# GLA's exponents as a pipe part of their own, and GLA and retention in one pipe

## The chip, the cores and the metric

The kernel runs on one core of one Trainium2 chip. The metric is the device time of one execution in microseconds (us). Three executions of the kernel before took 2648.84, 2644.02 and 2642.16 us; the median is 2644.02 us.

## The reference

Two transformer blocks on a sequence of 1024 rows of 1024 channels, in float32. The first block mixes tokens with two mixers side by side, retention (512 channels, 4 heads) and gated linear attention, GLA (512 channels, 4 heads with keys of 64), and then applies an MLP. The change touches the token mixer of this first block alone. Cut to what matters, GLA is, for each chunk of 64 rows:

```python
b = jnp.cumsum(lai, axis=1)
decay = jnp.exp(-jnp.abs(b[:, :, None] - b[:, None, :]))
A = jnp.einsum('bthd,bshd,btshd->bhts', qi, ki, decay)
o = jnp.einsum('bhts,bshe->bthe', A, vi)
o = o + jnp.einsum('bthd,bhde->bthe', qi * jnp.exp(b), state)
new_state = jnp.exp(b_last)[..., None] * state + jnp.einsum(
    'bshd,bshe->bhde', ki * jnp.exp(b_last[:, None] - b), vi)
```

The decay depends on the channel and on both rows, so it does not factor into one matmul. Both mixers end in a norm per head and a gate; the two results are put side by side and multiplied by `w_out`. The second block (SSD, S5 and RG-LRU mixers, cross attention, an MLP) is not touched.

## The kernel before

Every large product in float32 is made of three matmuls on split operands (`mm3`, L114 to L116: high by high, high by low, low by high), one for each 128 rows of the contraction, on a [128, 512] result. An operand is split by ACT (L82, a cast) and DVE (L83, the rest). Tiles come from pools with a fixed number of buffers (`BUFS`: 8 pages each of the kinds H and X, 8 of W, 4 of U, 6 of S; two PSUM tiles each of the kinds mm, tr and sc). The program is written as Python generators; the Tile framework takes the order in which instructions are written as their priority and fixes each engine's order by its own cost model. Engines wait for each other by semaphores, each engine keeps its own order, and so does each queue of DMAs.

The sequence is cut into 8 blocks of 128 rows. The stage of the change works so:

- `gla_proj` writes GLA's query, key and cumulated gate (`g_qkb`), its values (`gv`) and its output gate (`gg`) to DRAM.
- `ret_proj` makes retention's gate (`rg`, 8 tiles) and query and key (`r_qk`, 16 tiles) with 24 matmuls for each tile. It yields after every tile.
- `gla_block(i)` does one block of GLA in three parts. **Part one** loads values, gate and `g_qkb` (`vg`, `qkb`, pages H), and for j = 0, 1 makes seven levels of exponents: POOL subtracts (L562, seven instructions of 128x128), ACT takes the absolute value and the exponential (L564, L565, 128x896), DVE multiplies by the query (L567, into a second page X), POOL by the key (L568, in place). Then TensorE multiplies the levels (L575; two groups g = 0, 1 for each j, 16 matmuls of 64 rows each, into an sc tile), and DVE assembles the matrix A from the levels (L580 once and L583, a copy under a mask, 7 times for each j). **Part two** scales query and key for the state (L591 to L595), multiplies by the state and by A (L598, L600), transposes the keys (L604), copies them (L606, ACT), multiplies them with the values (L609) and updates the state (L614, DVE). Then it takes the norm's statistics (`head_norm`: L485, L486, small operations at L491, L492, L135 and L143 to L148, all on DVE) and scales the result (L503 on ACT). **Part three** gates it (L506, POOL), transposes it (L509, TensorE), scales it (L477, ACT) and writes it to DRAM (`g_od`).
- `pipe` starts one block more in each step and lets every live block do one part; it takes the newest block first unless `oldest` is set. `weave(main, side, n)` lets the side do n steps for each step of the main generator. Here the main is `ret_proj` and the side is the pipe of GLA blocks with n = 0.3.
- Behind it stand `ret_setup` (tables, and the weights of retention's values), a broadcast of the gate, `wout_load` (L703, POOL, and splits) and a second pipe, of `ret_block(i)`: its first part loads `r_qk` twice, makes the values with 24 matmuls, rotates (L662 POOL, L663 and L664 DVE), multiplies query by key (L668), masks (L669 DVE) and transposes (L673); its second part makes the output and the state (L679, L680, L682, L685), and norm and gate follow as in GLA.

A step below is the stretch from one block's first L575 to the next block's.

Of the kernel before, what the change touches and what calls it, by code (L numbers as in the profile page):

```python
# [17 lines left out]
NB = 8  # L18
# [377 lines left out]
def _rows(ap, t):  # L396
    return ap[t * 128:(t + 1) * 128, :]


class Mix1(Net):  # L400
# [110 lines left out]

    def pipe(self, gens, oldest=False):

        live, gens, d = [], list(gens), 1 if oldest else -1
        while gens or live:
            if gens:
                live.append(gens.pop(0))
            live = [g for g in live[::d] if next(g, self) is not self][::d]
            yield

# [26 lines left out]
    def gla_block(self, i):  # L547
        nc = self.nc
        sl = slice(128 * i, 128 * i + 128)
        vg = self.page("H")  # L550
        nc.sync.dma_start(out=vg[:, 0:512], in_=_rows(self.g_vd, i))
        nc.sync.dma_start(out=vg[:, 512:1024], in_=_rows(self.g_gd, i))
        qkb = self.page("H")[:, 0:768].rearrange("p (s j c) -> p s j c", s=3, c=128)
        nc.sync.dma_start(out=qkb, in_=self.g_qkb[:, :, :, sl])
        A = self.half([128, 2, 2, 128])
        for j in range(2):
            q, k, b = qkb[:, 0, j, :], qkb[:, 1, j, :], qkb[:, 2, j, :]
            E = self.page("X")[:, 0:896].rearrange("p (l c) -> p l c", c=128)
            for l in range(7):
                w = 64 >> l  # L560
                bv = b.rearrange("p (g c) -> p g c", c=2 * w)
                nc.gpsimd.tensor_tensor(out=E[:, l, :].rearrange("p (g c) -> p g c", c=2 * w), in0=bv,  # L562
                                        in1=bv[:, :, w - 1:w].broadcast_to([128, 64 // w, 2 * w]), op=ALU.subtract)
            nc.scalar.activation(out=E, in_=E, func=ACTF.Abs)  # L564
            nc.scalar.activation(out=E, in_=E, func=ACTF.Exp, scale=-0.0625)  # L565
            qt = self.page("X")[:, 0:896].rearrange("p (l c) -> p l c", c=128)
            nc.vector.tensor_tensor(out=qt, in0=E, in1=q.unsqueeze(1).broadcast_to([128, 7, 128]), op=ALU.mult)  # L567
            nc.gpsimd.tensor_tensor(out=E, in0=E, in1=k.unsqueeze(1).broadcast_to([128, 7, 128]), op=ALU.mult)  # L568
            for g in range(2):
                ps = self.ps("sc").rearrange("p (r u c) -> p r u c", r=2, c=128)  # L570
                for u in range(4):
                    l = 4 * g + u - 1
                    for r in range(2):
                        rs = slice(64 * r, 64 * r + 64)
                        nc.tensor.matmul(out=ps[:, r, u, :], lhsT=k[rs] if l < 0 else E[rs, l, :],  # L575
                                         rhs=q[rs] if l < 0 else qt[rs, l, :], start=True, stop=True)
                for u in range(4):
                    l = 4 * g + u - 1
                    if l < 0:
                        nc.vector.tensor_tensor(out=A[:, j], in0=ps[:, :, u, :], op=ALU.mult,  # L580
                                                in1=self.ident.unsqueeze(1).broadcast_to([128, 2, 128]))
                    else:
                        nc.vector.copy_predicated(out=A[:, j], data=ps[:, :, u, :],  # L583
                                                  mask=self.gmask[:, l, :].unsqueeze(1).broadcast_to([128, 2, 128]))
# [12 lines left out]
        for j in range(2):  # L597
            nc.tensor.matmul(out=o[:, 2 * j:2 * j + 2, :], lhsT=qd[:, j, :], rhs=self.g_S[j], start=True, stop=False)  # L598
            for h in (2 * j, 2 * j + 1):
                nc.tensor.matmul(out=o[:, h, :], lhsT=A[:, j, h % 2, :], rhs=vg[:, h * 128:(h + 1) * 128],  # L600
                                 start=False, stop=h % 2 == 1)
# [45 lines left out]
    def ret_block(self, i, T):  # L647
# [16 lines left out]
        nc.vector.tensor_tensor(out=qk, in0=qk, in1=sw, op=ALU.add)  # L664
        A, kT = sw[:, 0], sw[:, 1]
        ps = self.ps("tr").rearrange("p (h c) -> p h c", c=128)
# [1200 lines left out]
def build(tc, I, out):  # L1867
    from contextlib import ExitStack
    with ExitStack() as ctx:
        n = Mix2(tc, ctx, I, out)  # L1870
        n.modulation()
        n.kv_mem()
        def run(g):
            while True:
                try:
                    next(g)
                except StopIteration as e:
                    return e.value
# [7 lines left out]
        T, steps = None, [3, 0, 1, 0, 1]  # L1886
        while T is None:
# [4 lines left out]
            T = next(norm)  # L1892
# [5 lines left out]
            yield from n.s5_setup()  # L1898
        run(n.weave(n.gla_proj(T), early(), 0.75))
        n.gla_setup()  # L1900
        run(n.weave(n.ret_proj(T), n.pipe(n.gla_block(i) for i in range(NB)), 0.3))
        n.ret_setup()
        n.gate1 = n.bcast(n.mod["gate1"][0])
        n.wout = n.wout_load(I["w_out"], n.gate1, (4, 6))
        run(n.pipe(n.ret_block(i, T) for i in range(NB)))
        T = run(n.block1_out())
        T = n.block1_mlp(T)
        n.dt_proj(T)
# [9 lines left out]
        out = n.block2_out()  # L1918
        T = next(out)
        run(n.weave(n.pipe(n.ssd_block(i) for i in range(NB)), delay(out, 3)))  # L1920
        T = run(n.attention(T))
# [87 lines left out]
```

## Time and profile before

| what | value |
|---|---|
| median of three runs | 2644.02 us |
| the profiled execution | 2643.23 us, span 2641.4 us |
| TensorE busy, share of the span | 2536.1 us, 96% |
| mean granted TensorE clock | 0.982 |
| TensorE busy from 205 to 620 us | 370.82 of 415 us, clock 0.95 |
| TensorE busy from 620 to 2641 us | 1984.41 of 2021 us, clock 1.00 |

The stage of the change lies between about 300 and 620 us of the span. The granted clock has two levels here, 1.0 (2.4 GHz) and 0.5 (1.2 GHz); a value between them is the mean of a stretch that holds both.

### The profile page before, as it was taken

The numbers are of one execution on the slowest core, as the hardware profiler recorded it, in microseconds if no ns is written. First come the engines' busy times: TensorE is split into PE (matmuls) and PEld (weight loads), VectorE is DVE, ScalarE is ACT, GpSimd is POOL, SyncE is SP. The second block draws the span as 40 slices with busy tenths as digits, with TensorE's granted clock in tenths as the row PEclk, the third lists the DMA queues.
The fourth block names the chain that finished last, engine by engine and source line by source line (L and its number), as shares of the span: only waits on it lengthen the run. The fifth ranks groups of instructions, "written<-read, shape, count | busy, mean of one in ns | idle before, by whom it ended". The sixth has DMA issues, their size and how long they took to land. (4 is left out here: it accounts for less than half of the span.)

```text
span 2641.4 us, 32947 instructions
## 1 busy us (share of the span) xinstructions
PE 2536.1 (96%) x12086; PEld 2061.0 (78%) x12086; DVE 1877.5 (71%) x3177; ACT 1165.0 (44%) x1834; POOL 240.6 (9%) x222
## 2 busy tenths in 40 slices
PE   7899989889999999999999998999999999999997
PEld 7586777677888888888877776778887888888886
DVE  4857666688898777647775468786557977777786
ACT  3622233344654444433553474652227444434342
POOL 4121135541000000000000003100000000000000
PEclk8899999999999999999999999999999999999999
DMA  9772433465166569966632334371102765799783
GB/s 327 254 266 100 144 104 96 132 163 167 61 215 236 192 218 330 325 193 223 209 128 85 106 102 133 118 246 40 56 17 84 271 218 193 257 339 333 269 281 106
DMA packets 255130, 484.36 MB, mean 183 GB/s; under 512 B 21604, under 2 KB 110964, under 8 KB 254968
## 3 DMA queue, kind: packets, MB, share of 16 engines
q1 hardware_dynamic: 247768, 470.59, 52.6%
q10 hardware_dynamic: 7200, 11.67, 1.2%
q8 instruction: 95, 1.56, 0.2%
q14 instruction: 67, 0.55, 0.1%
HBM read 338.80 MB, written 143.38 MB: 183 GB/s over the span
## 5 line engine op out<-in xcount | busy, mean ns | idle before, releaser
L114 PE MATMUL ps<-W,H 128*128 128x512 f32 x1088 | 424.8, 390 | 0.3 <-ACT H L82 0.2
L116 PE MATMUL ps<-W,H 128*128 128x512 f32 x1088 | 424.2, 390 | 0.0
L115 PE MATMUL ps<-W,H 128*128 128x512 f32 x1088 | 423.9, 390 | 0.0
L83 DVE TENSOR_TENSOR W<-S,W 128x1024 fp32r<-128x1024 f32 (+1 forms) x271 | 332.2, 1230 | 127.6 <-ACT W L82 126.7
L114 PE MATMUL ps<-U,W 128*128 128x512 f32 (+1 forms) x1064 | 419.4, 394 | 2.5 <-ACT W L82 2.2
L115 PE MATMUL ps<-U,W 128*128 128x512 f32 (+1 forms) x1064 | 417.4, 392 | 1.5 <-DVE U L372 1.5
L116 PE MATMUL ps<-U,W 128*128 128x512 f32 (+1 forms) x1064 | 416.1, 391 | 0.8 <-DVE W L83 0.8
L82 ACT CAST W<-S 128x1024 fp32r<-128x1024 f32 x287 | 297.0, 1042 | 241.5 <-PE ps L115 155.4
L83 DVE TENSOR_TENSOR H<-S,H 128x1024 fp32r<-128x1024 f32 x131 | 159.9, 1221 | 150.3 <-ACT H L82 145.5
L82 ACT CAST H<-S 128x1024 fp32r<-128x1024 f32 x131 | 137.5, 1050 | 279.9 <-PE ps L115 197.9
L114 PEld LDWEIGHTS ps<-W,H 128*128 128x128 f32 x1088 | 204.3, 188 | 43.5 <-DVE X L1106 0.8
L114 PEld LDWEIGHTS ps<-U,W 128*128 128x128 f32 (+1 forms) x1064 | 197.0, 185 | 51.1 <-ACT W L82 3.4
L116 PEld LDWEIGHTS ps<-W,H 128*128 128x128 f32 x1088 | 204.2, 188 | 41.8
L115 PEld LDWEIGHTS ps<-W,H 128*128 128x128 f32 x1088 | 204.3, 188 | 41.6
L115 PEld LDWEIGHTS ps<-U,W 128*128 128x128 f32 (+1 forms) x1064 | 197.2, 185 | 48.3 <-DVE U L372 4.6
L116 PEld LDWEIGHTS ps<-U,W 128*128 128x128 f32 (+1 forms) x1064 | 197.0, 185 | 45.7 <-DVE W L83 1.9
L116 PE MATMUL ps<-W,U 128*128 128x512 f32 x352 | 140.7, 400 | 5.3 <-DVE U L83 5.3
L114 PE MATMUL ps<-W,U 128*128 128x512 f32 x352 | 142.3, 404 | 2.3 <-DVE X L305 2.0
L115 PE MATMUL ps<-W,U 128*128 128x512 f32 x352 | 141.2, 401 | 0.0
L807 ACT ACTIVATE ev<-ev 128x512 f32<-128x512 f32 x104 | 65.3, 629 | 135.2 <-DVE ev L905 110.3
L116 PEld LDWEIGHTS ps<-W,U 128*128 128x128 f32 x352 | 67.5, 192 | 20.7 <-DVE U L83 6.6
L808 ACT ACTIVATE X<-ev 128x512 f32<-128x512 f32 x126 | 79.8, 634 | 3.4
(546 smaller groups left out, 4523.3 us busy)
## 6 DMA issues: line engine op xcount, KB each, us to landing
S<-mlp_h SPq DMA_DIRECT2D x112, 512.0 KB, 5.0
S<-in_w_ff SPq DMA_DIRECT2D x96, 512.0 KB, 5.2
mlp_h<-X SPq DMA_DIRECT2D x96, 512.0 KB, 3.8
S<-in_mlp_w SPq DMA_DIRECT2D x96, 512.0 KB, 5.1
mlp_w<-S SPq DMA_DIRECT2D x96, 256.0 KB, 2.8
S<-mlp_w SPq DMA_DIRECT2D x48, 512.0 KB, 4.8
S<-in_w_in SPq DMA_DIRECT2D x46, 512.0 KB, 5.4
X<-in_w_ada SPq DMA_DIRECT2D x32, 512.0 KB, 6.8
```

The costliest lines, as they stand in the source:

```text
L82: self.nc.scalar.copy(out=hi, in_=src)
L83: (lo_eng or self.nc.vector).tensor_tensor(out=lo, in0=src, in1=hi.bitcast(F32), op=ALU.subtract)
L114: mm(out=ps, lhsT=lh, rhs=rh, start=start and k == 0, stop=False)
L115: mm(out=ps, lhsT=lh, rhs=rl, start=False, stop=False)
L116: mm(out=ps, lhsT=ll, rhs=rh, start=False, stop=stop and k == n - 1)
L807: nc.scalar.activation(out=r, in_=x, func=ACTF.Relu)
L808: nc.scalar.activation(out=out, in_=r, func=ACTF.Square)
```

## The change

`gla_block` gets four parts. The new first part loads `qkb` alone and makes the exponents and both products for j = 0 and 1, and keeps them in `Es`. The second part loads values and gate and holds the matmuls, now at L583, and the copies, now at L588 and L591. The other two parts are as they were. Lines behind the edit stand 8 further on in the changed program (L598 is L606, L604 is L612, L609 is L617, L595 is L603, L668 is L676, L673 is L681, L679 is L687); L506, L509, L562 to L568 stay.

`pipe` now takes its blocks from an iterator as it goes, and is called with `oldest` set. The two pipes are one: the generator `blocks` gives the eight GLA blocks, an empty one, then runs what is left of `ret_proj`, does the setups and `wout_load`, gives another empty one and then the eight retention blocks. It is woven with `ret_proj` at 0.42 in place of 0.3.

```diff
     def pipe(self, gens, oldest=False):
 
-        live, gens, d = [], list(gens), 1 if oldest else -1
-        while gens or live:
-            if gens:
-                live.append(gens.pop(0))
+        live, gens, d = [], iter(gens), 1 if oldest else -1
+        while True:
+            g = next(gens, None)
+            if g is not None:
+                live.append(g)
+            elif not live:
+                return
             live = [g for g in live[::d] if next(g, self) is not self][::d]
             yield
...
-        vg = self.page("H")
-        nc.sync.dma_start(out=vg[:, 0:512], in_=_rows(self.g_vd, i))
-        nc.sync.dma_start(out=vg[:, 512:1024], in_=_rows(self.g_gd, i))
         qkb = self.page("H")[:, 0:768].rearrange("p (s j c) -> p s j c", s=3, c=128)
         nc.sync.dma_start(out=qkb, in_=self.g_qkb[:, :, :, sl])
-        A = self.half([128, 2, 2, 128])
+        Es = []
...
+            Es.append((E, qt))
+        yield
+        vg = self.page("H")
+        nc.sync.dma_start(out=vg[:, 0:512], in_=_rows(self.g_vd, i))
+        nc.sync.dma_start(out=vg[:, 512:1024], in_=_rows(self.g_gd, i))
+        A = self.half([128, 2, 2, 128])
+        for j in range(2):
+            q, k, (E, qt) = qkb[:, 0, j, :], qkb[:, 1, j, :], Es[j]
...
-        run(n.weave(n.ret_proj(T), n.pipe(n.gla_block(i) for i in range(NB)), 0.3))
-        n.ret_setup()
-        n.gate1 = n.bcast(n.mod["gate1"][0])
-        n.wout = n.wout_load(I["w_out"], n.gate1, (4, 6))
-        run(n.pipe(n.ret_block(i, T) for i in range(NB)))
+        proj = n.ret_proj(T)
+
+        def blocks():
+            for i in range(NB):
+                yield n.gla_block(i)
+            yield iter(())
+            run(proj)
+            n.ret_setup()
+            n.gate1 = n.bcast(n.mod["gate1"][0])
+            n.wout = n.wout_load(I["w_out"], n.gate1, (4, 6))
+            yield iter(())
+            for i in range(NB):
+                yield n.ret_block(i, T)
+
+        run(n.weave(proj, n.pipe(blocks(), True), 0.42))
```

DVE before, in the third block's step (X_3141 and X_3180 are the products of that block's successor, `half_2887` is the matrix A that is assembled, `ps_2901` to `ps_2953` are its four groups):

```order
L148 SCALAR_TENSOR_TENSOR sm_2743<-rs_2744,sm_2743 128x4
L567 TENSOR_TENSOR X_3141<-X_3131,H_3128 128x896
L567 TENSOR_TENSOR X_3180<-X_3170,H_3128 128x896
L580 TENSOR_TENSOR half_2887<-ps_2901,ident 128x256
L583 COPY_PREDICATED half_2887<-half_2298,ps_2901 128x256 x3
L583 COPY_PREDICATED half_2887<-half_2298,ps_2914 128x256 x4
L580 TENSOR_TENSOR half_2887<-ps_2940,ident 128x256
L583 COPY_PREDICATED half_2887<-half_2298,ps_2940 128x256 x3
L583 COPY_PREDICATED half_2887<-half_2298,ps_2953 128x256 x2
```

DVE now, in the same block's step (`half_2948` is its A, `ps_2962` to `ps_2988` are its last three groups, X_3216 and X_3229 are products of the block two further on):

```order
L591 COPY_PREDICATED half_2948<-half_2298,ps_2962 128x256 x2
L588 TENSOR_TENSOR half_2948<-ps_2975,ident 128x256
L591 COPY_PREDICATED half_2948<-half_2298,ps_2975 128x256
L567 TENSOR_TENSOR X_3216<-X_3206,H_3204 128x896
L591 COPY_PREDICATED half_2948<-half_2298,ps_2975 128x256 x2
L591 COPY_PREDICATED half_2948<-half_2298,ps_2988 128x256 x4
L567 TENSOR_TENSOR X_3229<-X_3219,H_3204 128x896
L83 TENSOR_TENSOR W_3505<-S_3503,W_3504 128x1024
L83 TENSOR_TENSOR W_3511<-S_3509,W_3510 128x1024
L485 BN_STATS st_3122<-ps_3104 128x6 x2
```

The two products moved from ahead of the copies of the block before them into the copies of the block two before them, and ahead of a norm's statistics.

POOL before, two neighbouring steps (H_2966, H_3209 and H_3452 at L506 are the gated outputs, H_3371 and H_3642 are two blocks' `qkb`):

```order
L506 TENSOR_TENSOR H_2966<-H_2966,H_2620 128x512
L595 TENSOR_TENSOR H_3209<-H_3209,H_2885 128x256
L562 TENSOR_TENSOR X_3374<-H_3371 128x128 x7
L562 TENSOR_TENSOR X_3413<-H_3371 128x128 x7
L568 TENSOR_TENSOR X_3374<-X_3374,H_3371 128x896
L568 TENSOR_TENSOR X_3413<-X_3413,H_3371 128x896
L595 TENSOR_TENSOR H_3452<-H_3452,H_3128 128x256
L506 TENSOR_TENSOR H_3209<-H_3209,H_2882 128x512
```

POOL now, one step (H_3447 at L603 belongs to the block after the one in L506's turn, H_3893 is the last block's `qkb`):

```order
L603 TENSOR_TENSOR H_3785<-H_3785,H_3447 128x256
L506 TENSOR_TENSOR H_3554<-H_3554,H_3391 128x512
L562 TENSOR_TENSOR X_3895<-H_3893 128x128 x7
L568 TENSOR_TENSOR X_3895<-X_3895,H_3893 128x896
L562 TENSOR_TENSOR X_3908<-H_3893 128x128 x7
L568 TENSOR_TENSOR X_3908<-X_3908,H_3893 128x896
```

Where both sets of subtractions stood ahead of both products, the second set now stands behind the first product, and all of them behind L506.

TensorE before, the matmuls of the levels in one step (U and W are operands of `ret_proj`):

```order
L575 MATMUL ps_3144<-H_3128 128x128 x2
L575 MATMUL ps_3144<-X_3141,X_3131 128x128 x6
L575 MATMUL ps_3157<-X_3141,X_3131 128x128 x8
L604 MATMUL ps_3224<-ident,H_3209 128x128 x2
L114 MATMUL ps_3272<-U_613,W_3058 128x512
L575 MATMUL ps_3183<-H_3128 128x128 x2
L575 MATMUL ps_3183<-X_3180,X_3170 128x128 x6
L575 MATMUL ps_3196<-X_3180,X_3170 128x128 x8
```

TensorE now, from the last of twelve matmuls of `ret_proj` behind the first group (`ps_3165`, `ps_3178` and `ps_3191` are the other three groups of the same block):

```order
L115 MATMUL ps_3244<-U_614,W_3233 128x512
L583 MATMUL ps_3165<-X_3013,X_3003 128x128 x8
L583 MATMUL ps_3178<-H_3001 128x128 x2
L583 MATMUL ps_3178<-X_3026,X_3016 128x128 x6
L116 MATMUL ps_3244<-U_613,W_3234 128x512
L114 MATMUL ps_3244<-U_613,W_3239 128x512
L115 MATMUL ps_3244<-U_614,W_3239 128x512
L583 MATMUL ps_3191<-X_3026,X_3016 128x128 x8
```

The single matmul between the two j became twelve between the groups of j = 0, none between j = 0 and j = 1, and three between the groups of j = 1. Between one block's first group and the next block's stood 96, 72, 72, 96, 72 and 7 of these matmuls from the second block on, and now 48, 48, 72, 48, 72 and 48. The first L676 of retention stands behind the last GLA block's products with the state, as L668 did.

## Rows read from the trace of the kernel before

**Rows 1.** Busy time by windows of the span; columns as the first line says.

```profile
core 0: us, PE busy (x) PEld busy (x) DVE busy (x) ACT busy (x) POOL busy (x), PEclk, DMA share, GB/s
205.00:620.00 415.00, 370.82 (x2149) 302.21 (x2148) 290.03 (x831) 143.55 (x301) 144.06 (x151) 0.95 0.42 128
620.00:2641.00 2021.00, 1984.41 (x9059) 1613.33 (x9057) 1460.34 (x2180) 936.97 (x1426) 35.73 (x26) 1.00 0.54 185
```

**Rows 2.** TensorE's waits, 205 to 620 us: total us, times, longest.

```profile
PE ps L575 <- DVE half L583: 23.2, 11, 6.9
PE ps L668 <- DVE H L664: 4.3, 3, 2.2
```

**Rows 3.** Timeline from 380 us: start, us, engine, line, operation, [idle before <-releaser].

```profile
379.91 0.39 PE L116 MATMUL ps<-U,W 128*128 128x512 f32 x1
380.14 0.39 PE L114 MATMUL ps<-U,W 128*128 128x512 f32 x1
...
381.78 5.11 POOL L562 TENSOR_TENSOR X<-H 128x128 f32<-128x128 f32 x14 [5.32 <-DMA H<-g_qkb]
...
386.76 1.09 DVE L567 TENSOR_TENSOR X<-X,H 128x896 f32<-128x896 f32 x1 [9.21 <-ACT X L565]
...
387.93 2.08 POOL L568 TENSOR_TENSOR X<-X,H 128x896 f32<-128x896 f32 x1 [1.03 <-DVE X L567]
...
388.96 1.99 DVE L567 TENSOR_TENSOR X<-X,H 128x896 f32<-128x896 f32 x1 [1.12 <-ACT X L565]
...
392.86 0.80 PE L575 MATMUL ps<-H 64*128 64x128 f32 x4 [4.53 <-DVE half L583]
```

**Rows 4.** Windows as in 1: a long wait and the stretch behind it, thrice.

```profile
387.90:392.80 4.90, 0.43 (x3) 0.11 (x1) 3.65 (x5) 1.80 (x3) 3.85 (x2) 0.75 0.14 54
392.80:397.10 4.30, 4.24 (x33) 3.88 (x34) 3.67 (x9) 0.00 (x0) 0.30 (x1) 0.50 0.00 0
418.60:422.50 3.90, 0.44 (x3) 0.12 (x1) 3.70 (x5) 0.58 (x2) 3.90 (x2) 0.82 0.61 202
422.50:427.90 5.40, 5.35 (x35) 4.80 (x36) 4.43 (x10) 0.00 (x0) 4.71 (x3) 0.50 0.01 3
480.50:487.50 7.00, 0.52 (x3) 0.20 (x2) 6.90 (x7) 3.17 (x5) 4.27 (x3) 0.89 0.40 121
487.50:492.80 5.30, 4.92 (x25) 4.06 (x25) 4.62 (x10) 0.80 (x4) 4.20 (x2) 0.50 0.55 179
```

**Rows 5.** Window as in 1: one step without a long wait.

```profile
360.00:386.00 26.00, 24.64 (x163) 20.31 (x163) 14.19 (x41) 8.14 (x19) 7.61 (x15) 1.00 0.33 107
```

**Rows 6.** Groups: busy us, mean ns of one | idle before, releasers.

```profile
L506 POOL TENSOR_TENSOR H<-H,H 128x512 f32<-128x512 f32 x16 | 23.4, 1462 | 39.9 <-ACT H L503 23.9 <-ACT H L500 16.0
L562 POOL TENSOR_TENSOR X<-H 128x128 f32<-128x128 f32 x91 | 35.2, 426 | 90.2 <-PE ps L575 61.6 <-DMA H<-g_qkb 16.3 <-DVE s5t L1467 12.3
L564 ACT ACTIVATE X<-X 128x896 f32<-128x896 f32 x12 | 11.4, 953 | 44.3 <-POOL X L562 44.3
L567 DVE TENSOR_TENSOR X<-X,H 128x896 f32<-128x896 f32 x12 | 18.3, 1527 | 51.8 <-ACT X L565 51.8
L583 DVE COPY_PREDICATED half<-half,ps 128x256 f32<-128x256 uint8 x112 | 49.4, 443 | 5.7 <-PE ps L575 1.7
L485 DVE BATCH_NORM_STATS2 st<-ps 128x6 f32<-128x128 f32 x32 | 8.0, 287 | 0.1
L491 DVE TENSOR_TENSOR sm<-sm 128x4 f32<-128x4 f32 x8 | 1.3, 157 | 0.0
L503 ACT ACTIVATE H<-ps,sm 128x128 f32<-128x128 f32 x25 | 7.2, 369 | 5.8 <-DVE sm L148 5.8
L83 DVE TENSOR_TENSOR W<-S,W 128x1024 fp32r<-128x1024 f32 x12 | 18.9, 1584 | 6.2 <-ACT W L82 6.2
```

**Rows 7.** DMA issues, 300 to 620 us: times, KB each, median us to landing.

```profile
g_od<-H SPq DMA_DIRECT2D x8, 256.0 KB, 3.0
H<-g_qkb SPq DMA_DIRECT2D x5, 384.0 KB, 5.2
```

## The prediction

> **What bounds the kernel now.** I read the windows of busy time first, then TensorE's waits inside the stretch they point to, then the timeline around the longest of them. From 620 us on TensorE is busy 1984.4 of 2021 us at full clock, so nothing is to be had there; from 205 to 620 us it is busy 370.8 of 415 us at a clock of 0.95 [rows 1]. Those 44.2 idle us and the half clock are all that this change can touch. More than half of the idle time is one wait: L575, the matmuls of GLA's levels, for L583, the copies that free its PSUM tile, 23.2 us in 11 waits, the longest 6.9 [rows 2].
>
> The copies are not slow themselves. In the timeline POOL begins the next block's subtractions at 381.78, late because its `qkb` had only just landed. ACT's functions follow, DVE makes the next block's product of j = 0 from 386.76 and that of j = 1 until 390.95. Only then may DVE copy the groups of the present block, for which TensorE has been waiting, since DVE's order puts both products ahead of the copies; TensorE goes on at 392.86 after 4.53 us [rows 3]. So a late exponent stops TensorE not as an operand, for it is the next block's, but through the copies queued behind it. This happens three times. The three waits leave 4.90 - 0.43 = 4.47, 3.90 - 0.44 = 3.46 and 7.00 - 0.52 = 6.48 us idle, and behind each of them TensorE runs at a granted clock of 0.50, the lower of the two levels, for 4.24, 5.35 and 4.92 busy us, half of which is lost [rows 4]. A step without such a wait stands at full clock throughout [rows 5].
>
> **What is removed.** The three waits and the half clock behind them: 14.4 + (4.24 + 5.35 + 4.92) / 2 = 14.4 + 7.3 = 21.7 us [rows 4]. In the new order the copies of j = 0 stand ahead of both products, so a late exponent no longer holds the groups that TensorE wants next; I count all of it as gone. The eight shorter waits that make up the rest of the 23.2 us, some 8 us, may shrink, as twelve matmuls now cover the first group's copies; but where the ring below sets the step that pays nothing, so I count none of it and keep 8 us as the bound.
>
> **What is added: a loop over the engines.** The new DVE order puts L567 of block k+2 amid the copies of block k and ahead of the norm's statistics, and the new POOL order puts the subtractions of k+2 behind L506 of block k-1, the second set behind L568 of the first. That closes a ring with one turn for each step: statistics on DVE, L503 on ACT, L506, L562, ACT, L567, L568, L562, ACT, L567, statistics. Its length by the means [rows 6]: the DVE tail is 26 instructions, 8 for the statistics at up to 0.287, 8 copies and state updates at up to 0.443, 10 small ones from 0.157, 7.4 us at these prices, and I take 7.0 since the statistics' second kind is shorter; L503 4 x 0.369 = 1.48; L506 1.46; seven L562 at 0.426 = 2.98, twice; ACT 2 x 0.953 = 1.91, twice; L567 1.53, twice; L568 2.08 [rows 3]. The sum is 24.9 us. With the shortest that the timeline shows, L562 at 5.11 / 14 = 0.365 and L567 at 1.09 [rows 3], it is 23.1. I take 24.0, the middle, since L562 and L567 will run in part alone.
>
> TensorE's own step: the undisturbed one took 26.0 us with 72 matmuls of `ret_proj` [rows 5]. These follow each other by 380.14 - 379.91 = 0.23 us [rows 3], so a step with 48 takes 26.0 - 24 x 0.23 = 20.5. The steps in which exponents are still made have 48, 48, 72, 48 and 72. In the three short ones the ring is longer by 24.0 - 20.5 = 3.5 us, together 10.5. If the two long ones' slack of 2.0 each could be used it would be 5 x 24.0 - (3 x 20.5 + 2 x 26.0) = 6.5. I take 8.5. By the ends of the ring, 23.1 and 24.9, this term runs from 2.0 to 13.2.
>
> In two of the five steps a pair of weight splits (L83) stands behind the second L567 and ahead of the statistics, 2 x 1.58 = 3.2 us more in the ring [rows 6]; it counts in full in the second step (48 matmuls) and less 2.0 of slack in the fifth (72): 4.4 us. In the second step the wait so becomes 3.5 + 3.2 = 6.7 us, longer than two of the three waits behind which the half clock stood; I charge it one such stretch, half of 5.35, 2.7 us [rows 4].
>
> What row is there on who holds DVE? L567 took 1.09 us alone and 1.99 us where it began while POOL's L568, from 387.93 to 390.01, was under way; it ended 0.94 us behind it [rows 3]. The Trainium skill (SBUF — State Buffer, "SBUF: two separate sides") says that a VectorE operation with two SBUF inputs and a GpSimd operation take one shared port pair as a lock for the whole instruction. The trace agrees. By that rule L567 would always run alone in the new order, as L568 waits for it, the ring would stand near its short end, 23.1, and the sum below would be some 2.7 us better, an estimate. The same rule speaks against the change at the splits, which now follow L567 at once and so run beside L568: up to 2.08 us more in each of two steps, some 4 us worse, and together 1 us worse than my sum.
>
> **What is only moved.** Loading values and gate in the second part moves two DMAs of 256 KB on SP's queue behind `qkb`; they are wanted a step later, at L608, and cost nothing while SP isn't blocked. Retention's first L676 still stands behind the last GLA block's output, so the single pipe weaves little. In retention's blocks two matmuls of the values, not some twenty, now stand between transposes and L687, which exposes the mask on DVE. The bounds are a gain of the 4.3 us that L668 waits for L664 now [rows 2] and a loss of 8 x 0.7, the copy of one group and more, 5.6 us; I take nothing, as both lie about equally near.
>
> **The sum**: 21.7 - 8.5 - 4.4 - 2.7 = 6.1 us gained. Against the profiled execution, 2643.2, this is 2637.1 us; the median of the runs is 0.8 higher, and I forecast 2637.5. That lies at the edge of what a measurement of this kernel can tell from no change, about 0.3% or 7.9 us.
>
> **Rivals.**
> 1. *The ring never binds.* POOL need not wait for L506 where the statistics came early, and a step's lead is spent before the ring catches up. Then the 21.7 us are gained in full, and half of the eight short waits' 8 us: 2643.2 - 25.7 = 2617.5 us. For it: DVE is idle for 51.8 us in front of L567 today, all for ACT [rows 6], time which the new order could fill. Against it: the new order is a chain with few gaps.
> 2. *Slower: the load of `qkb` ends last.* POOL already stood 16.3 us for `qkb` [rows 6]. The page for block k+2's `qkb` comes free when block k-2 has been written out, on the same SP queue: 3.0 + 5.2 = 8.2 us from one issue to the other's landing [rows 7]. If that lands behind L506 of step k by 4.5 us, somewhat less than the 5.32 that POOL stood idle ahead of 381.78 [rows 3], the ring grows to 28.5 and, as L567 stands in the copies, TensorE stops with it: 5 x 4.5 = 22.5 us, 2660 us. It decides from the point at which the load lands later than L506 begins. Against it: a whole group of matmuls stands between the block's last transpose and the next step.
> 3. *The change doesn't do what it says*: the exponents gain a step, but DVE's and POOL's fixed orders hand the wait on one to one, and nothing is woven. Then waits of 3 to 7 us stay in other places: 2640 to 2648, say 2644 us.
>
> **How the numbers follow.** Forecast 0.50, within it 2629 to 2647 from the bounds of the ring and of retention; rival 1 0.20; rival 2 0.13; rival 3 0.17. Faster than 2636.1: rival 1 and a little under half of the forecast, 0.20 + 0.24 = 0.44. Slower than 2651.9: rival 2 and a little of the others, 0.15. Between: 0.41. The range reaches half into rival 1 and not to rival 2's full price: 2616 to 2655 us leaves out about one in ten on each side.
>
> **What would show it.** In the changed profile L567 should no longer wait some 10 us for ACT with TensorE idle; the wait of L583 for L591 should be shorter than 23.2 us and without the three long ones; the clock behind a block's first groups should be 1.00, not 0.50. The ring is right if steps with 48 matmuls take about 24 us and those with 72 about 26. Steps of 20.5 us would show rival 1; POOL idle in front of L562 for `qkb` in every step, and steps of 28 us, rival 2. An unchanged sum of idle time, in other waits, would show rival 3. I would be wrong altogether if the time moved outside 300 to 620 us.

## The result, and the profile after

The changed kernel took 2661.88 us (median of four runs, 2659.29 to 2664.44) against 2643.64 us before: a ratio of 1.0067, with a 95% interval of 1.0055 to 1.0080. It is slower by 18 us. The forecast was 6 us faster, and the time lies above the top of the stated range, 2655 us.

The windows say where. The columns are those of [rows 1]; first the changed kernel, then the kernel before.

```profile
300.00:520.00 220.00, 197.26 (x1183) 154.96 (x1182) 145.45 (x349) 75.30 (x145) 95.01 (x119) 0.95 0.35 113
520.00:640.00 120.00, 98.52 (x543) 82.78 (x542) 73.57 (x209) 45.60 (x121) 39.98 (x24) 0.93 0.59 152
640.00:1000.00 360.00, 359.65 (x1602) 294.46 (x1601) 297.81 (x510) 180.48 (x279) 0.00 (x0) 1.00 0.51 178
```

```profile
300.00:520.00 220.00, 194.49 (x1209) 159.38 (x1207) 140.55 (x354) 72.96 (x138) 97.13 (x118) 0.95 0.35 114
520.00:640.00 120.00, 106.25 (x604) 89.46 (x605) 91.98 (x247) 52.62 (x138) 42.16 (x25) 0.97 0.65 178
```

Behind 640 us TensorE is busy at full clock, as it was before [rows 1], so what was lost was lost ahead of it: in GLA's stretch 26 fewer matmuls in the same 220 us, and in retention's 61 fewer in 120 us, at a mean clock of 0.93 in place of 0.97. The long waits of [rows 2] are gone, and others stand in their place. TensorE's waits in the changed kernel from 205 to 640 us (total us, times, longest):

```profile
PE ps L509 <- POOL H L506: 19.7, 9, 3.3
PE ps L617 <- ACT H L614: 6.7, 3, 3.1
PE ps L583 <- DVE half L591: 6.6, 10, 1.6
PE ps L617 <- DVE half L622: 5.4, 7, 2.0
```

Two of them can be followed on the timeline (start, us, engine, line, operation). In GLA, the transposes of the keys (L612) are done, and the state matmul L617 stands on TensorE's queue almost behind them; but the copy L614 that it needs stands on ACT behind two casts, a copy for the projection and the four scalings of the block before:

```profile
377.06 1.98 ACT L82 CAST W<-S 128x1024 fp32r<-128x1024 f32 x2
...
377.27 1.09 DVE L567 TENSOR_TENSOR X<-X,H 128x896 f32<-128x896 f32 x1 [4.30 <-ACT X L565]
...
377.55 0.38 PE L612 MATMUL ps<-ident,H 128*128 128x128 f32 x2
...
377.86 0.49 PE L583 MATMUL ps<-H 64*128 64x128 f32 x4
...
378.27 4.23 DVE L83 TENSOR_TENSOR W<-S,W 128x1024 fp32r<-128x1024 f32 x2
378.44 2.99 POOL L568 TENSOR_TENSOR X<-X,H 128x896 f32<-128x896 f32 x1 [3.58 <-DVE X L567]
378.95 0.58 ACT L640 COPY ev<-ps 128x512 f32<-128x512 f32 x1
...
379.98 0.88 ACT L477 ACTIVATE H<-ps,norm_w 128x128 f32<-128x128 f32 x3 [0.18 <-issue]
...
380.75 0.38 ACT L614 COPY H<-ps 128x256 f32<-128x256 f32 x1
...
381.18 0.70 PE L617 MATMUL ps<-H,H 128*128 128x256 f32 x2 [2.39 <-ACT H L614]
...
384.92 1.22 PE L617 MATMUL ps<-H,H 128*128 128x256 f32 x2 [1.97 <-DVE half L622]
```

TensorE is busy 1.75 of the 3.70 us that follow, and then runs at the lower clock for most of a stretch (columns as before, the clock is third from the end):

```profile
381.20:384.90 3.70, 1.75 (x9) 0.98 (x9) 3.55 (x15) 0.00 (x0) 0.22 (x1) 0.77 1.00 362
384.90:391.00 6.10, 6.08 (x26) 4.61 (x28) 3.19 (x13) 1.84 (x6) 2.00 (x2) 0.58 0.55 180
```

In retention, ACT has scaled the output (L500) by 582.98, but POOL does L670 of a later block first, which itself had waited for its load, and only then the gate L506; TensorE's order has the transposes L509 as the next thing:

```profile
581.48 1.50 ACT L500 ACTIVATE H<-ps,sm,sm 128x128 f32<-128x128 f32 x4 [0.32 <-DVE sm L496]
...
582.46 2.35 POOL L670 TENSOR_TENSOR H<-H,half 128x1024 f32<-128x1024 f32 x1 [1.04 <-DMA H<-r_qk]
...
584.77 1.26 POOL L506 TENSOR_TENSOR H<-H,H 128x512 f32<-128x512 f32 x1
...
586.09 0.66 PE L509 MATMUL ps<-ident,H 128*128 128x128 f32 x4 [2.34 <-POOL H L506]
```

For the comparison of the variants below I count TensorE's work: each matmul with its undisturbed spacing (0.2275 us for one of `mm3`, 0.0605 for one of 64 rows, 0.1115 and 0.217 for 128x128 and 128x256), summed in the order of each trace. The table gives how much later than the kernel before each profiled execution had done the same sum, in us. At 520 us the order of the work still differs a little, so the middle column is good to a few us; the last one is firm.

| kernel | at 300 us | at 520 us | at 640 us | median, ratio to before |
|---|---|---|---|---|
| changed | -1.7 | +7.4 | +17.9 | 2661.9, 1.0067 |
| e2_oldest | +0.2 | +24.4 | +28.5 | 2673.0, 1.0109 |
| e3_split | -0.8 | +3.6 | +13.5 | 2657.0, 1.0048 |
| e4_ret_before | -1.5 | +8.8 | +5.2 | 2646.6, 1.0008 |
| e5_mixed | -0.5 | +4.8 | -0.4 | 2647.0, 1.0012 |
| e8_rotdve | -2.0 | +7.5 | +1.4 | 2645.6, 1.0004 |
| e1_newest | -0.7 | -0.4 | -5.2 | 2639.9, 0.9985 |
| e9_two_new | -0.3 | +3.3 | +1.9 | 2640.6, 0.9986 |
| i3_rot | -0.4 | +1.5 | -8.9 | 2634.6, 0.9957 |
| j1_rot_before | +0.2 | -2.2 | -2.4 | 2641.8, 0.9988 |

The profiled execution of a kernel may lie some us off its median (that of e4_ret_before 7 us above, that of e9_two_new 5), so verdicts go by the medians and ratios.

### The profile page after: what moved, and what is told of

The parts are those of the page before. It is cut to its first block, busy times and chain, and to the rows that moved or that the text cites. A ratio compares the mean times of both kernels' runs of the same rounds, so it can differ in the third digit from the quotient of the medians.

```text
span 2661.7 us, 32935 instructions
## 1 busy us (share of the span) xinstructions
PE 2550.2 (96%) x12086; PEld 2064.7 (78%) x12086; DVE 1882.4 (71%) x3177; ACT 1165.4 (44%) x1834; POOL 239.9 (9%) x222
## 4 chain that ended last, share of the span: by engine, by line
PE 66%; DVE 6%; ACT 2%; DMA 1%; issue 1%; DVEq 0%; ACTq 0%
PE ps L116 21%; PE ps L114 21%; PE ps L115 21%; PE ps L182 1%; DVE st L155 1%; DVE bc L1261 0%; PE ps L1716 0%; DVE U L83 0%; DMA H<-s_xbc 0%; ACT H L171 0%; PE ps L218 0%; PE ps L1750 0%; PE ps L1343 0%; DVE W L83 0%; DVE half L1330 0%
## 5 line engine op out<-in xcount | busy, mean ns | idle before, releaser
L83 DVE TENSOR_TENSOR W<-S,W 128x1024 fp32r<-128x1024 f32 (+1 forms) x271 | 329.8, 1220 | 130.2 <-ACT W L82 129.0
L82 ACT CAST W<-S 128x1024 fp32r<-128x1024 f32 x287 | 297.6, 1043 | 242.4 <-PE ps L115 148.9
L83 DVE TENSOR_TENSOR H<-S,H 128x1024 fp32r<-128x1024 f32 x131 | 160.7, 1227 | 151.8 <-ACT H L82 147.1
L82 ACT CAST H<-S 128x1024 fp32r<-128x1024 f32 x131 | 137.6, 1050 | 283.4 <-PE ps L115 199.9
L116 PEld LDWEIGHTS ps<-W,U 128*128 128x128 f32 x352 | 67.9, 193 | 20.3 <-DVE U L83 6.3
```

Of the source, the lines that this page charges most:

```text
L82: self.nc.scalar.copy(out=hi, in_=src)
L83: (lo_eng or self.nc.vector).tensor_tensor(out=lo, in0=src, in1=hi.bitcast(F32), op=ALU.subtract)
L116: mm(out=ps, lhsT=ll, rhs=rh, start=False, stop=stop and k == n - 1)
```

## Experiments: which part of the change costs the time

The change has four parts: the exponents as a part of their own, oldest block first, one pipe for both mixers, and the ratio 0.42. I held three theories: **O**, the order oldest first is the cost; **S**, the exponents' own part with its ring over the engines is; **W**, the single pipe and its ratio are.

**e1_newest.** One word undone:

```diff
-        run(n.weave(proj, n.pipe(blocks(), True), 0.42))
+        run(n.weave(proj, n.pipe(blocks()), 0.42))
```

> The changed kernel with one word undone: the single pipe takes the newest block first, as both pipes did before. Theory O (the oldest-first order puts the state matmuls L617 right behind the transposes whose copy L614 they need, and retention's L509 too soon behind L506): the L617 waits of 12 us and the L509 waits of 20 us both fall below 5 us, and the time comes to 2635 to 2646 us. Theory S (the exponents as a part of their own cost the time, through the ring over DVE, ACT and POOL): the time stays at 2655 to 2662. Theory W (the single pipe and the ratio 0.42 cost it): also 2655 to 2662, with the L509 waits still there.

Measured 2639.9 us, ratio 0.9985 (0.9974 to 0.9996): the whole loss is gone, and 4 us more. TensorE waits 0.4 us at L617 and 3.0 us for L506. Theory O holds, S and W fall as the main cause.

**e2_oldest.** The kernel before, with the order alone changed:

```diff
-        run(n.weave(n.ret_proj(T), n.pipe(n.gla_block(i) for i in range(NB)), 0.3))
+        run(n.weave(n.ret_proj(T), n.pipe((n.gla_block(i) for i in range(NB)), True), 0.3))
...
-        run(n.pipe(n.ret_block(i, T) for i in range(NB)))
+        run(n.pipe((n.ret_block(i, T) for i in range(NB)), True))
```

> The kernel before with both pipes set to oldest first, and nothing else of the change: three parts, two pipes, ratio 0.3. Theory O: L609 waits for L606 and for the state update as in the changed kernel, 8 us or more, L509 waits for L506 10 us or more, and the time is 2652 to 2668 us. Theories S and W: 2640 to 2648, as before.

Measured 2673.0 us, ratio 1.0109: the order alone costs 28 us in the old kernel, more than the whole change, and 5 us above theory O's range. But the waits are not all the ones I named: L509 waits 9.5 us for L506, and most of the rest is L575 waiting for the copies (17.9 us) and for L503 of the block before (13.8 us), which I had not expected; L609 waits for the updates 2.2 us only.

**e3_split** and **e9_two_new.** The four-part block with two pipes, newest first; e3 with the ratio 0.3, e9 with 0.42. In both, in place of the changed kernel's lines:

```diff
+        run(n.weave(n.ret_proj(T), n.pipe(n.gla_block(i) for i in range(NB)), 0.3))
+        n.ret_setup()
+        n.gate1 = n.bcast(n.mod["gate1"][0])
+        n.wout = n.wout_load(I["w_out"], n.gate1, (4, 6))
+        run(n.pipe(n.ret_block(i, T) for i in range(NB)))
```

> The changed kernel's four-part GLA block, with the two pipes, newest first, and the ratio 0.3 of before. Theory O: the long waits for copies behind L567 are gone and nothing comes in their place, 2625 to 2642 us. Theory S: the ring shows in the steps, 2655 or more. Theory W: 2638 to 2648.

> GLA in four parts, newest first, ratio 0.42, then the setups and a separate pipe for retention, newest first: e1_newest without the single pipe, or e3_split with 0.42 for 0.3. If the single pipe matters little: 2637 to 2643 us, as e1_newest, and e3_split's 2657 is then the ratio's doing, because at 0.3 the last GLA blocks stand behind the end of the projection's matmuls. If the single pipe is what saves e1_newest: 2650 to 2660 us.

Measured 2657.0 us (1.0048) for e3 and 2640.6 us (0.9986) for e9. e3 lies in theory S's range, not in O's, and e9 tells why. A block now needs one step of the pipe more, while `ret_proj` yields 24 times: at 0.3 that is 7 steps for 8 blocks, so the last blocks' matmuls are left for when the projection's have run out. TensorE's order shows it: the longest runs of a projection's matmuls ahead of or among the last two blocks' groups are 15 and 13 in e3, and 68 and 44 in e9. At 0.42 there are 10 steps. The ratio is worth 16 us once the block has four parts; the single pipe is worth nothing (e9 against e1_newest, 0.7 us).

**e4_ret_before** and **e5_mixed.** The changed kernel with retention newest first; in e4 in a pipe of its own, in e5 within the single pipe. The edit shown is e5's:

```diff
+            n.d = -1
             for i in range(NB):
                 yield n.ret_block(i, T)
...
-        live, gens, d = [], iter(gens), 1 if oldest else -1
+        live, gens, self.d = [], iter(gens), 1 if oldest else -1
...
+            d = self.d
             live = [g for g in live[::d] if next(g, self) is not self][::d]
```

> The changed kernel with retention taken out of the single pipe: GLA in four parts, oldest first, ratio 0.42, then the setups and a pipe of retention's blocks newest first, as before. Theory O: the GLA stretch loses what it loses in the changed kernel (L617 waits about 12 us), retention's L509 waits fall from 20 us below 5 us: 2648 to 2655 us. Theory S: 2655 to 2662, since GLA is unchanged and retention is not the cause. Theory W: 2640 to 2650.

> The changed kernel with its single pipe and 0.42, GLA's blocks oldest first as changed, but from retention's first block on the pipe takes the newest first. Against the changed kernel this differs in retention's order alone, against e1_newest in GLA's order alone. If the order of retention is its cost (theory R): L509's wait for L506 falls from 20 us to below 8 and the time is 2643 to 2650 us, as with e4_ret_before. If it is the single pipe that costs retention its time (theory W): 2655 to 2662 us, and e4_ret_before was better only for its separate pipe.

Measured 2646.6 and 2647.0 us (1.0008 and 1.0012). e4 came out below theory O's range and within W's; but e5, which keeps the single pipe, takes the same time, so it is the order of retention, worth 15 us, and again the single pipe is worth nothing. What is left between e5_mixed and e1_newest, 7 us, is the order of GLA's blocks alone. In e5 the waits of GLA stand as in the changed kernel, those of retention are small (its lines are one further on, L618 is L617):

```profile
PE ps L618 <- ACT H L615: 7.6, 3, 3.2
PE ps L584 <- DVE half L592: 6.7, 11, 1.7
PE ps L618 <- DVE half L623: 5.5, 7, 2.5
...
PE ps L509 <- POOL H L506: 4.9, 5, 1.8
```

So 18 us slower is 15 us of retention's order and 7 us of GLA's, less 4 us of gain.

## Experiments: the waits themselves

**e8_rotdve.** The changed kernel, but POOL need not do L670 ahead of the gate:

```diff
-        nc.gpsimd.tensor_tensor(out=v8(qk), in0=v8(qk), in1=b8(0), op=ALU.mult)
+        nc.vector.tensor_tensor(out=v8(qk), in0=v8(qk), in1=b8(0), op=ALU.mult)
```

> The changed kernel with retention's first rotation product L670 on DVE in place of POOL, so that POOL has only L678 and the gate L506 for each block of retention. Theory P (L506 comes late because POOL has to do L670, which waits for its load, first): L509's wait for L506 falls from 20 us to below 8, and the time to 2650 to 2657 us in spite of 8 x 1.2 us more on DVE. Rival (the norm's chain on DVE and ACT is late itself): the wait stays above 15 us, 2660 to 2672 us.

Measured 2645.6 us (1.0004): 16 us back, below theory P's range and as much as by retention's order, although DVE has eight operations more. POOL now does L506 as soon as ACT has scaled, and the longest wait of L509 is 1.4 us:

```profile
575.14 1.27 POOL L506 TENSOR_TENSOR H<-H,H 128x512 f32<-128x512 f32 x1 [1.64 <-ACT H L500]
...
576.46 0.66 PE L509 MATMUL ps<-ident,H 128*128 128x128 f32 x4 [0.63 <-POOL H L506]
```

Theory P holds: in retention it takes both, oldest first, which lets TensorE's order have L509 next, and the late L506 on POOL. The scheduler also moved some of L509 with this edit, so the 16 us are those of the edit with its new order.

**e6_ufirst.** The changed kernel, with both state matmuls ahead of the updates:

```diff
+        for j in range(2):
             for r in range(2):
```

> The changed kernel with GLA's two state matmuls L617 written ahead of the four state updates L622, so that the second matmul no longer waits for the updates from the first half of the same PSUM tile; all else as changed. Theory U (these waits cost their 5.4 us and the half clock behind them): L617 waits for DVE below 1 us, 2654 to 2658 us. Rival (the steps are set by the ring over DVE, ACT and POOL, and the wait turns up elsewhere): 2659 to 2663.

Measured 2662.8 us (1.0067), no gain. The wait of L617 for L622 is gone, and the copies' grew by as much:

```profile
PE ps L509 <- POOL H L506: 21.5, 9, 3.9
PE ps L583 <- DVE half L591: 12.6, 12, 4.1
PE ps L617 <- ACT H L614: 4.4, 2, 3.3
```

So the waits at L617 are how the lost time shows in the oldest-first order, and taking away half of them gives nothing; theory U falls. GLA's 7 us are shown for the order as a whole, not for one of its waits.

## Experiments: where the expected gain went

With the order newest first the earlier exponents should have been worth some 20 us; e1_newest gives 4. Its waits in the stage:

```profile
PE ps L606 <- DVE half L591: 11.8, 6, 6.5
PE ps L583 <- DVE half L591: 10.8, 13, 1.9
```

The copies on DVE hold TensorE for 11.8 + 10.8 = 22.6 us, as much as the 23.2 us of [rows 2]; only it is now the output L606 that waits, for the copies of its own block, because L567 of the block two further on stands among them and waits for ACT. The half clock came along: after the longest wait it is what [rows 4] show, 5.46 busy us at 0.50:

```profile
434.00:440.50 6.50, 0.07 (x1) 0.00 (x0) 2.33 (x5) 2.93 (x6) 3.28 (x7) 0.67 0.31 95
440.50:446.00 5.50, 5.46 (x17) 4.76 (x18) 3.25 (x10) 2.17 (x3) 3.26 (x8) 0.50 0.12 35
```

Three runs take L567 off DVE's order, and two more make the ring wider.

**h1_qtpool**, **h5_qt_before**, **h7_qt_after.** L567 on POOL, in e1_newest, in the kernel before and in the changed kernel:

```diff
-            nc.vector.tensor_tensor(out=qt, in0=E, in1=q.unsqueeze(1).broadcast_to([128, 7, 128]), op=ALU.mult)
+            nc.gpsimd.tensor_tensor(out=qt, in0=E, in1=q.unsqueeze(1).broadcast_to([128, 7, 128]), op=ALU.mult)
```

> e1_newest (the changed kernel, newest first throughout) with the query product L567 on POOL in place of DVE, so that nothing in DVE's order waits for the exponents any more. Theory Q (in e1_newest the wait of L606 for the copies L591, 12 us, and the half clock behind it come from L567 standing in DVE's order amid the copies and waiting for ACT): L606's wait falls below 3 us, 2625 to 2634 us. Rival (POOL, with 2 x 2.1 us more for each block, becomes late for the gate L506 and the ring stays as long): the time stays at 2637 to 2645 with waits of L509 or L583 in place of L606.

> The kernel before with the query product L567 on POOL in place of DVE, and nothing of the change. If the three long waits of L575 for the copies come from L567's place ahead of them in DVE's order, as the reading of the trace of before has it: L575's waits fall from 23 us below 12, none above 2 us, and the time by 12 to 22 us, 2622 to 2632 us. If the exponents themselves are late for TensorE as an operand, or POOL becomes late: 2636 to 2648 us with waits of the same length.

> The changed kernel, oldest first, with L567 on POOL in place of DVE. Theory Q' (the ring through L567 on DVE sets GLA's steps in the changed kernel too): the GLA stretch shortens by 5 to 12 us, 2650 to 2657 us. Theory O (in the changed kernel GLA loses its time to the place of the state matmuls L617 behind the copy L614, which this does not move): within 3 us of the changed kernel, 2658 to 2664 us, with L617's waits of 12 us still there.

Measured 2648.1 (1.0011), 2661.3 (1.0060) and 2682.2 us (1.0138): worse by 7, 16 and 19 us (by the ratios) than the kernel each was made from. None gained, as the rivals had it, but all three lie above every range that I had given. In e1_newest with L567 on POOL the wait of L606 is gone (11.8 us became 0.4), as theory Q had it, so there L567's place did hold the copies; but others make up for it: L583 for the copies rose from 10.8 to 13.4 us, and a matmul of the projection waits 8.1 us for ACT. In the kernel before, L575's waits stayed where they were, now with one of 11 us:

```profile
PE ps L575 <- DVE half L583: 23.5, 11, 11.0
```

On POOL the exponents, both products and, for the last blocks, the scaling of `w_out` now stand behind each other, and a product takes 2.1 us here against 1.09 on DVE:

```profile
424.55 2.11 POOL L567 TENSOR_TENSOR X<-X,H 128x896 f32<-128x896 f32 x1 [2.12 <-ACT X L565]
```

And the copies still depend on the exponents, by another way. ACT's cast of a weight (L82) stands behind the exponents' function L564, which waits for POOL; on DVE the rest of that split (L83) waits for the cast, and the copies stand behind L83. This is the longest wait:

```profile
498.81 0.95 ACT L564 ACTIVATE X<-X 128x896 f32<-128x896 f32 x1 [6.36 <-POOL X L562]
499.67 1.03 ACT L82 CAST W<-S 128x1024 fp32r<-128x1024 f32 x1
...
500.73 1.23 DVE L83 TENSOR_TENSOR W<-S,W 128x1024 fp32r<-128x1024 f32 x1 [19.46 <-ACT W L82]
...
505.35 2.44 DVE L583 COPY_PREDICATED half<-half,ps 128x256 f32<-128x256 uint8 x5
...
506.90 0.80 PE L575 MATMUL ps<-H 64*128 64x128 f32 x4 [11.01 <-DVE half L583]
```

From 300 to 520 us DVE waits 52.0 us at L83 for L82, where it waited 6.2 us in the kernel before. So h5_qt_before took away one link between the exponents and the copies, and another one held; it does not decide what L567's place alone cost the kernel before. To move L567 frees nothing in any of the three, since the exponents stay late in whichever queue they stand. That their chain takes about a step is what I take from this; no run shows it by itself.

**i1_s4** and **i2_x10s4.** e1_newest with fewer pages S as a control, and the same with two more pages X for the exponents (the edit shown is i2's; i1 keeps X=8):

```diff
-    BUFS = dict(U=4, X=8, H=8, W=8, S=6, half=6, ev=4, bc=3)
+    BUFS = dict(U=4, X=10, H=8, W=8, S=4, half=6, ev=4, bc=3)
```

> A control: e1_newest with 4 pages S in place of 6, which makes room for the next run. S holds what is loaded before it is split, so this can delay weights. Expected 0 to 8 us above e1_newest, 2640 to 2648 us, with GLA's stretch as in e1_newest.

> i1_s4 with 10 pages X in place of 8: the exponents and products of half a block more fit. In e1_newest POOL's first subtractions for block k+2 wait for TensorE's L583 of block k, whose pages they take. Theory X (these pages close the ring, and so eat what the earlier exponents would have given): L562's wait for TensorE goes, L606's wait for the copies falls from 12 us below 6, and the time is 4 to 12 us below i1_s4. Rival (the chain of L562, ACT, L567 and L568 is long enough by itself): within 3 us of i1_s4.

Measured 2708.8 and 2722.5 us (1.0236 and 1.0293). The control missed its forecast by 60 us: the four pages S cost it ahead of 300 us and far behind, from 1000 us on, where nothing else was touched; up to 640 us it stood 2.4 us behind the kernel before. Within GLA the comparison still holds. First i1, then i2:

```profile
PE ps L583 <- DVE half L591: 13.2, 16, 1.9
PE ps L606 <- DVE half L591: 11.9, 7, 5.7
```

```profile
PE ps L583 <- DVE half L591: 20.9, 14, 4.8
...
PE ps L606 <- DVE half L591: 5.9, 7, 1.6
```

L606's wait fell to half, as theory X had it, and L583's rose by more: 25.1 us in all became 26.8, and i2 stood 10.9 us behind the kernel before at 640 us, where theory X had a gain. More room moves the wait from the block's end to the next block's start, and TensorE loses no less. With the newest first, the pages are not what binds.

**h2_qtpool_rot**, **i3_rot**, **j1_rot_before**, **j2_rot_u**, **i4_elast_rot.** The edit of e8_rotdve, L670 on DVE, on top of h1_qtpool, of e1_newest and of the kernel before; then i3_rot with e6_ufirst's edit, and i3_rot with the block just started taken last in each step of the pipe:

```diff
-            live = [g for g in live[::d] if next(g, self) is not self][::d]
+            order = live[:-1][::-1] + live[-1:]
+            done = [g for g in order if next(g, self) is self]
+            live = [g for g in live if g not in done]
```

> h1_qtpool with retention's first rotation product L670 on DVE in place of POOL. Theory P (POOL's order holds back the gate L506 in retention also when the newest block goes first): 2 to 6 us below h1_qtpool, L509's wait below 2 us. Rival (DVE is the tighter engine there; L676 waits for L672 on DVE): 0 to 6 us above h1_qtpool.

> e1_newest with retention's first rotation product L670 on DVE. Theory P (POOL's queue in retention costs time there also with the newest first): 2 to 6 us below e1_newest, 2634 to 2638 us. Rival (DVE is as tight as POOL there): 2638 to 2644.

> The kernel before with retention's first rotation product (L662 there) on DVE, and nothing of the change: what of i3_rot's gain needs the changed GLA. If the gain is retention's alone: 2635 to 2639 us, 5 to 9 us below before. If i3_rot's gain comes from the parts together: 2640 to 2646.

> i3_rot with GLA's two state matmuls written ahead of the four state updates, as in e6_ufirst. With the newest first sixteen matmuls stand between the transposes and the state matmuls, so nothing should wait there: within 3 us of i3_rot, 2632 to 2638 us. If the scheduler's new order of L606 and L509 behind them frees the copies: 2626 to 2631.

> i3_rot with one more change of the pipe: the parts of the blocks already under way go newest first, and the part of the block just started, GLA's exponents or retention's loads and scores, goes last. If it is the exponents' rank ahead of the norm and the gate of the block before that makes the ring: L606's wait falls below 6 us, 2628 to 2636 us. If retention's first part suffers from standing last, as with oldest first, L676 or L509 wait more: 2640 to 2650 us.

h2 took 2644.0 us (0.9994), 4 us below h1. i3_rot took 2634.6 us, ratio 0.9957 (0.9942 to 0.9972), below both kernels; j1_rot_before 2641.8 (0.9988), j2_rot_u 2637.0 (0.9969), which is no better than i3_rot, and i4_elast_rot 2662.8 (1.0066). Of i4's loss some 20 us arise after 1500 us, where the second block's SSD mixer uses the same pipe; ahead of 700 us it stands level with the kernel before, 9 us behind i3_rot. So it tells that this rank is no better, not that it is 28 us worse there. The wait of the output (L606 in i3_rot) fell from 11.1 to 0.2 us, as forecast, and that of the next groups (L583 there) rose from 10.7 to 19.3: the wait moved once more. The windows of i3_rot, to be read beside the two at the head of this part:

```profile
300.00:520.00 220.00, 190.88 (x1208) 155.87 (x1206) 149.00 (x362) 78.22 (x155) 91.91 (x120) 0.97 0.37 119
520.00:640.00 120.00, 112.05 (x643) 95.51 (x643) 92.07 (x270) 51.63 (x128) 20.34 (x16) 1.00 0.61 174
```

GLA's stretch does the work of the kernel before, no more, and the gain is in retention, 643 matmuls for 604 at full clock. j1_rot_before has retention's edit without the new GLA and gains 3 us of the 11. So the parts of the change are worth 8 us (0.9957 against 0.9988) once oldest first is taken out and POOL relieved, against the 21.7 us that the prediction put down.

## Why the prediction was wrong

Between the forecast, 6 us gained, and the result, 18 us lost, lie 24 us. Some 15 of them are retention's, which the sum put at nothing. The other 9 are GLA's: e5_mixed, with GLA as changed and retention in its old order, is 3 us slower than the kernel before (1.0012), where the sum has 6 us gained.

**The bound held, and the reading of [rows 2 to 4] in the main.** Nearly all that moved lies between 300 and 640 us, 17.9 us of the 20.3 between the two spans. With L567 moved, the three long waits went, as forecast, and L583's wait for the copies fell from 23.2 to 6.6 us. But L567's place is one way by which a late exponent holds the copies, and h5_qt_before showed another, through the casts.

**The term that was mis-sized first: 21.7 us "counted as gone".** The waits did not go, they changed place. Even with the order that suits it (e1_newest) TensorE waits 22.6 us for the same copies, at L606 and L583. I removed a wait without asking what would be late next for the same reason: the exponents' chain through POOL, ACT and DVE takes most of a step, and whichever matmul follows its last product waits. That the chain is so long is argued; that the wait moves on to the next matmul is what e1_newest, i2_x10s4 and i4_elast_rot show.

**The ring did not set the steps.** I put it at 24.0 us and so the steps with 48 matmuls of the projection at 24, those with 72 at 26. The starts of the first groups of four blocks (L583, `qkb` as an operand; the second block's was at 330.65):

```profile
352.47 0.49 PE L583 MATMUL ps<-H 64*128 64x128 f32 x4
...
411.69 0.49 PE L583 MATMUL ps<-H 64*128 64x128 f32 x4
433.90 0.49 PE L583 MATMUL ps<-H 64*128 64x128 f32 x4
467.49 0.49 PE L583 MATMUL ps<-H 64*128 64x128 f32 x4
```

Two of the short steps took 21.8 and 22.2 us, less than the ring's short end of 23.1 and nearer to TensorE's own 20.5. The third took 25.4 us, from 352.47 to the 377.86 shown further up: TensorE waited 1.18 us at L617 for L614 and from 357 to 363 us ran at a mean clock of 0.53. The splits that I had charged to this step ran from 378.27, in the next one. The long ones took 411.69 - 377.86 = 33.8 and 467.49 - 433.90 = 33.6 us, some 7.7 us above my 26, and TensorE's largest waits in them are not where the ring's price had them. Both begin with L614 late on ACT, TensorE waiting at L617 and then running at the lower clock. In the first it is the casts of the splits that stand ahead of L614, as shown, and the splits on DVE hold up the statistics and L622; in the second it is the exponents' own functions:

```profile
433.69 0.95 ACT L564 ACTIVATE X<-X 128x896 f32<-128x896 f32 x1 [6.26 <-POOL X L562]
...
437.26 0.38 ACT L614 COPY H<-ps 128x256 f32<-128x256 f32 x1
...
437.69 1.17 PE L617 MATMUL ps<-H,H 128*128 128x256 f32 x2 [3.08 <-ACT H L614]
```

I had priced splits and exponents in the ring alone, and not in the queue ahead of L614. In the changed trace six or ten matmuls of 64 rows stand between the transposes L612 and the first L617; before, 32 of them and one of the projection stood between L604 and L609 in the first five of these steps. The prediction does not speak of this move.

**Retention at nothing.** This was the largest miss, 15 us by e4_ret_before, e5_mixed and e8_rotdve, against bounds of -4.3 and +5.6. I looked at the mask between transposes and L687, which cost nothing that shows: L687's waits sum to 1.0 us. L509 was the place: its wait for L506 rose from 3.6 to 19.7 us. The prediction named L506 as a member of GLA's ring and did not ask where oldest first puts L509 in retention, nor what POOL has to do ahead of L506 there.

**The rivals.** Rival 2 gave 2660 us, nearly the time, by a mechanism that did not happen: POOL's idle time ahead of L562 names TensorE in the changed kernel and `qkb` nowhere from 300 to 520 us. Rival 1's gain did not come, though the two undisturbed short steps were nearer to its 20.5 us than to the ring's 24. Rival 3's second half came true, as e9_two_new shows: the single pipe weaves nothing. Its first half, the wait handed on one to one, is what e1_newest shows, where 23.2 us became 22.6; the changed kernel came out above its 2648 us by the order that it does not name. No rival named the change of order, the one word `True`, and it carries the whole loss.

**The rule on the port.** In the changed kernel eleven of the twelve L567 took 1.09 us, as at 377.27, with POOL waiting for it; the twelfth took 2.20 us beside POOL's L711. The two splits from 378.27 took 4.23 us beside L568, which took 2.99. Both agree with the rule of the Trainium skill (SBUF — State Buffer, "SBUF: two separate sides") by which an operation of DVE with two SBUF inputs and one of POOL take one shared port pair as a lock. What it was worth in the time no run shows; the prediction had it at 1 us.

**The sum.** As written, 2637.1 + 0.8 gives 2637.9 and not 2637.5; nothing hangs on it.

**What stays open.** Why GLA loses 7 us by oldest first is shown for the order and not for one wait: taking away half of L617's waits gave nothing. And of the ring's parts I tried the place of L567, the pages and the rank of the exponents, the last two with the newest first alone, each without a gain; that the chain's own length binds is what they leave, and no run shortened it.

## What to carry to other kernels

Where a scheduler keeps the written order as priority, the order in which a pipe takes its live blocks is a change of every engine's queue, and it deserves its own price: look for the matmul that moves up to just behind what it depends on, and for what else the engine in between has in its queue. A wait that is taken away can come back at the producer's next consumer, as 23.2 us at one group of matmuls came back here as 22.6 at two; compare the sum of all waits for one producer, not one wait. And a new part in a pipe needs the weaving ratio to match, or the last blocks run bare.

## What the runs showed that I had not expected

POOL looks idle, 9% busy over the span, and yet moving one product of each pair to it made three kernels slower by 7 to 19 us: the multiply of 128x896 took 2.1 us there and 1.09 on DVE when it ran alone, and other engines waited for POOL's queue. And two pages of staging fewer cost some 60 us in parts of the kernel that the study had not looked at.
